# The rounded part and the rest of the softmax heads' norm factor, formed on GpSimd instead of VectorE

## The chip, the cores and the metric

The kernel runs on one core of one Trainium2 chip. The metric is device time of one execution in microseconds (us); lower is better. The engines are TensorE (PE in the profile; PEld is its weight load), VectorE (DVE), ScalarE (ACT), GpSimd (POOL) and SyncE (SP, which here only issues transfers). Each engine works through its own instructions in a fixed order.

## The reference, cut to what matters

Two layers over 512 tokens of width 1024. Each layer has eight stick-breaking heads and four heads of differential softmax attention side by side, then an output projection and an MLP with a squared ReLU. The part that matters here is the norm behind the four softmax heads:

```python
df_heads = differential_attention(dq, dk, dvv, lam)          # 4 heads of width 128
df_out = (rmsnorm(df_heads, subln_norm[l]) * (1.0 - lambda_init)).reshape(B, S, DF_WIDTH)
# rmsnorm: x * rsqrt(mean(x*x, axis=-1) + EPS) * g
```

and the rotation of the softmax heads' queries and keys, `rope`, which works in two halves of each head: one comes out as a difference of two products, the other as a sum.

## The kernel before, in words

**Layout and precision.** Activations stand transposed, channels on the 128 partitions and the 512 tokens along the row. Matmuls run in a rounded fp32 type (fp32r). To keep the precision, an operand is held as two tiles, a rounded part ("hi") and the rest ("lo"): ScalarE makes hi (`split`, L224; weights L116), VectorE subtracts it from the original to make lo (L225; weights L117). A dense product is then three matmuls (`three`, L281 to L283).

**Order of the work.** In each layer one stream of dense matmuls (the input projection, block after block, then the output projection of the softmax half) is interleaved on TensorE, in an order that is worked out when the program is built, with the attention pieces: the scores of one unit (L477, L478), the transposes of an older unit's weights (`s2`, L567) and the value products of a still older one (`s3`). TensorE takes them in exactly that order; a matmul whose operand is late holds up everything behind it. The framework's scheduler then places the instructions on the other engines by its own priorities, so that the order there is not always that of the source. The order on POOL is what matters below.

**The norm of a softmax head** (eight of them, heads 0 to 3 of two layers) has two halves. `start_norm` (L638) calls `rms_a` (L244) with GpSimd as `eng`: TensorE transposes the squares (L248); VectorE sums them (`ms`, L249) and adds the floor (L253); GpSimd raises the four columns to the power -1/2 (`rc`, L259, 128x4); VectorE rounds them (`chi`, L260) and subtracts (`clo`, L261); GpSimd spreads the columns onto two diagonals of 128x512 (`dghd`, L264, and `dgld`, L266). One stage later `finish` (L646) calls `rms_b`, where two matmuls broadcast the diagonals over the partitions (`rb_d`, L274 and L275), ScalarE copies the result (L276), and GpSimd multiplies the head's output by it (L650). `rms_a` is also called for the norm in front of the input projection, with VectorE as `eng`.

**The rotation of head 3** falls into the same stretch as the norm of an earlier head. VectorE multiplies the projection's result by cosines and sines (`u`, `v`, L445 and L446). GpSimd forms the sum (`v0d3q`, L454) and the difference (`u0d3q`, L453). Each is split (ScalarE L224 makes hi, VectorE L225 makes lo, both in tile `hl0d3k`), and SP moves the pieces by small transfers into the stacked operands of the scores (L420): hi into `st0d3k`, lo into `kl0d3k`, both into `st0d3q`. SP also issues the weight loads (L99) in its one order. In layer 1 the names have a 1 in place of the 0.

**Weights.** While TensorE works on a block, the next block's weights are split: ScalarE makes `whi` (L116), VectorE makes `wlo` (L117, 128x1024 from two tiles in SBUF).

Of the kernel before, what the change touches and what calls it, by code (L numbers as in the profile page):

```python
# [9 lines left out]
F32 = mybir.dt.float32  # L10
# [141 lines left out]
def trunk(ctx, tc, xT, w, w2, gains, gfin, lamv, cos, sin, out):  # L152
    nc = tc.nc
# [8 lines left out]
    def bank(tag, name):  # L162
        if tag == "any":
            tag = ("mm", "s", "s", "mm", "s")[turn[0] % 5]
            turn[0] += 1
        return ps.tile([P, 512], F32, tag=tag, name=name, bufs=banks[tag])
# [49 lines left out]
    chi = cp.tile([P, 4], F32R, tag="chi", name="chi")  # L216
    clo = cp.tile([P, 4], F32, tag="clo", name="clo")
# [26 lines left out]
    def rms_a(src, inv_n, col, name, eng, dgt, floor=None):  # L244
        pt = bank("t", "rs_" + name)
        if RST and eng is not nc.gpsimd or RST == 2:
            for j in range(4):
                nc.tensor.transpose(pt[:, j * P : (j + 1) * P], src[:, j * P : (j + 1) * P], ident)  # L248
            nc.vector.tensor_reduce(out=ms, in_=pt.rearrange("p (j f) -> p j f", j=4), axis=AX.X, op=ALU.add)  # L249
            if floor is None:  # L250
                nc.vector.tensor_scalar(out=ms, in0=ms, scalar1=inv_n, scalar2=EPS, op0=ALU.mult, op1=ALU.add)
            else:
                nc.vector.scalar_tensor_tensor(  # L253
                    out=ms, in0=ms, scalar=inv_n, in1=floor, op0=ALU.mult, op1=ALU.add)
        else:
            for j in range(4):
                nc.tensor.matmul(pt[:, j : j + 1], src[:, j * P : (j + 1) * P], ones, start=True, stop=True)
            nc.vector.tensor_scalar(out=ms, in0=pt[:, 0:4], scalar1=inv_n, scalar2=EPS, op0=ALU.mult, op1=ALU.add)
        nc.gpsimd.tensor_tensor(out=col, in0=ms, in1=mhalf, op=ALU.pow)  # L259
        nc.vector.tensor_copy(chi, col)  # L260
        nc.vector.tensor_sub(clo, col, chi.bitcast(F32))  # L261
        dg_hi, dg_lo = dgt("dgh" + name), dgt("dgl" + name)
        idb = ident.unsqueeze(1).to_broadcast([P, 4, P])
        eng.tensor_mul(  # L264
            dg_hi.rearrange("p (j t) -> p j t", j=4), idb, chi.bitcast(F32).unsqueeze(2).to_broadcast([P, 4, P]))
        eng.tensor_mul(  # L266
            dg_lo.rearrange("p (j t) -> p j t", j=4), idb, clo.unsqueeze(2).to_broadcast([P, 4, P]))

        return dg_hi, dg_lo
# [47 lines left out]
    for l in range(L):  # L317
        with ExitStack() as actx:
# [319 lines left out]
            def start_norm():  # L638
                b, os_, sqo, rc = late[0]
                floor = a3.tile([P, 4], F32, tag="floor", name=f"floor{l}{b}")  # L640
                nc.vector.scalar_tensor_tensor(
                    out=floor, in0=tops[b], scalar=EPS, in1=tops[b], op0=ALU.mult, op1=ALU.mult)
                dgs[b] = rms_a(sqo, 1.0 / P, rc, f"d{l}{b}", nc.gpsimd, tr, floor)
                return 0.43
# [65 lines left out]
            def dense(pts):  # L710
                if l == 0:
                    us = [W.next("x"), W.next("x")]
                    pts = [bank("mm", f"p{l}{i}") for i in range(2)]
                    turns = [(c, i) for c in range(5) for i in range(2)] + [(c, i) for i in range(2) for c in (5, 6, 7)]
                    for c, i in turns:
                        three(pts[i], wpair(us[i], c), hpair(c), c == 0, c == KC - 1)
                        yield 3 * 0.216
                step, b = 2 * KC, int(ORDER[0][1])
                held = [(pts[0], "d", b, "q"), (pts[1], "d", b, "k")]
                for item in ORDER[1:]:  # L720
                    kind, b = item[0], int(item[1])
                    for which in ("qk" if kind in "ds" else "v"):
                        name = f"p{l}{kind}{b}{which}"
                        for pt in block(name, "s" if step in (16, 24, 32) else "mm"):
                            step += 1
                            if step == RA[l]:
                                dgs["a"] = rms_a(ssq, 1.0 / D, rcol, f"a{l}", nc.vector, tr)
                            if step == RB[l]:
                                rms_b(rbc, f"a{l}", dgs["a"])
                                nc.vector.tensor_mul(cos_t, cos_t, rbc)  # L730
                                nc.vector.tensor_mul(sin_t, sin_t, rbc)
                            yield 3 * 0.216
                        held.append((pt, kind, b, which))
                        if step >= RB[l]:
                            for args in held:
                                {"w": evict_v, "u": evict_v, "s": evict_s, "d": evict_d}[args[1]](*args)
                            held = []
                yield from wo(1)
# [375 lines left out]
```

## Time and profile before

| what | us |
|---|---|
| median of 3 runs | 1173.97 |
| the 3 runs | 1173.69 to 1174.61 |
| the profiled execution, its own time | 1170.51 |
| its span, first to last instruction | 1168.7 |
| mean granted TensorE clock | 0.997 |

The span is what the views of the profile cover; 1.8 us of the profiled execution lie around it. A row of the timeline gives the start, the duration, engine, line, operation, what is written and what is read, shape and count, and, in brackets, how long the engine was idle just before and what ended that. An engine with a q behind its name (SPq) is the sequencer that issues a transfer. A row of the waits gives who waited for whom, the sum in us, the number of times and the longest.

### The profile page before, as it was taken

How to read it: one execution, taken by the hardware profiler on the slowest of the kernel's cores; microseconds unless marked ns; L12 is line 12 of the kernel's file. 1: busy time of each engine (PE TensorE's matmuls, PEld its weight loads, DVE VectorE, ACT ScalarE, POOL GpSimd, SP SyncE). 2: the span in 40 equal slices, each digit the busy share in tenths (PEclk: the TensorE clock that was granted, in tenths of full speed). 3: DMA queues.
4: the chain of work that ended last, by engine and by line, in shares of the span. 5: the costliest groups of instructions: out<-in, count | busy, mean ns of one | idle time of the engine just before them, and what ended most of it. 6: DMA issues, size and time to landing. Idle time of an engine off the chain costs nothing.

```text
span 1168.7 us, 15328 instructions
## 1 busy us (share of the span) xinstructions
PE 1147.7 (98%) x5454; PEld 952.0 (81%) x5454; DVE 813.0 (70%) x1302; ACT 652.4 (56%) x1153; POOL 213.7 (18%) x282
## 2 busy tenths in 40 slices
PE   9999999999999999999899999999999999999996
PEld 6887888888888888888688878888888888888884
DVE  7888788765545756647789877877655466476568
ACT  6455666556756446455445556655666563554554
POOL 1222443130100101002012215331201010010021
PEclk9999999999999999999999999999999999999999
DMA  7555433255844936837525553432658368276185
GB/s 246 163 151 171 123 113 109 72 190 152 212 136 105 224 128 126 224 95 157 110 72 166 168 153 109 140 96 73 225 122 229 120 124 226 93 168 192 36 173 132
DMA packets 56860, 170.11 MB, mean 146 GB/s; under 512 B 7120, under 2 KB 8144, under 8 KB 56784
## 3 DMA queue, kind: packets, MB, share of 16 engines
q1 hardware_dynamic: 46416, 131.88, 34.6%
q0 software_dynamic: 10224, 37.23, 18.5%
q8 instruction: 43, 0.70, 0.2%
q14 instruction: 33, 0.27, 0.1%
q10 hardware_dynamic: 144, 0.02, 0.0%
HBM read 138.17 MB, written 2.10 MB: 120 GB/s over the span
## 4 chain that ended last, share of the span: by engine, by line
PE 86%; DVE 5%; DMA 2%; issue 2%; ACT 1%; POOL 0%; SPq 0%; POOLq 0%; DVEq 0%; ACTq 0%
PE f L282 10%; PE f L283 10%; PE f L281 10%; PE x L282 4%; PE x L281 4%; PE x L283 4%; PE wo L281 3%; PE wo L282 3%; PE wo L283 3%; DMA q<-in_w 2%; DVE wlo L117 1%; PE T0s L567 1%; PE T1s L567 1%; PE O0s L596 0%; PE O1s L596 0%
## 5 line engine op out<-in xcount | busy, mean ns | idle before, releaser
L117 DVE TENSOR_TENSOR wlo<-raw,whi 128x1024 fp32r<-128x1024 f32 (+1 forms) x130 | 154.6, 1193 | 98.0 <-ACT whi L116 97.4
L117 DVE TENSOR_TENSOR wlo<-q,whi 128x512 fp32r<-128x512 f32 x224 | 146.0, 687 | 106.2 <-ACT whi L116 105.7
L281 PE MATMUL f<-h_hi,whi 128*128 128x512 f32 x512 | 199.6, 390 | 0.0
L283 PE MATMUL f<-h_hi,wlo 128*128 128x512 f32 x512 | 199.3, 389 | 0.0
L282 PE MATMUL f<-h_lo,whi 128*128 128x512 f32 x512 | 199.2, 389 | 0.0
L116 ACT ACTIVATE whi<-q 128x512 fp32r<-128x512 f32 x224 | 129.6, 624 | 120.3 <-PE f L282 38.1
L116 ACT ACTIVATE whi<-raw 128x1024 fp32r<-128x1024 f32 (+1 forms) x130 | 131.5, 1018 | 106.7 <-PE f L282 55.4
L794 POOL DMA_DIRECT2D q<-in_w x64 | 56.0, 878 | 558.1 <-DVE wlo L117 471.9
L281 PEld LDWEIGHTS f<-h_hi,whi 128*128 128x128 f32 x512 | 96.1, 188 | 19.9
L282 PEld LDWEIGHTS f<-h_lo,whi 128*128 128x128 f32 x512 | 96.1, 188 | 19.9
L283 PEld LDWEIGHTS f<-h_hi,wlo 128*128 128x128 f32 x512 | 96.1, 188 | 19.9
L225 DVE TENSOR_TENSOR Al<-F,Ah 128x256 fp32r<-128x256 f32 (+2 forms) x96 | 74.8, 779 | 44.1 <-ACT Ah L224 44.0
L281 PE MATMUL x<-whi,Ah 128*128 128x512 f32 x256 | 100.0, 391 | 0.0
L282 PE MATMUL x<-wlo,Ah 128*128 128x512 f32 x256 | 99.8, 390 | 0.1
L283 PE MATMUL x<-whi,Al 128*128 128x512 f32 x256 | 99.7, 389 | 0.0
L224 ACT ACTIVATE Ah<-F 128x256 fp32r<-128x256 f32 (+2 forms) x96 | 67.6, 704 | 45.7 <-DVE F L830 43.7
L282 PEld LDWEIGHTS x<-wlo,Ah 128*128 128x128 f32 x256 | 48.1, 188 | 10.4 <-DVE wlo L117 0.5
L281 PEld LDWEIGHTS x<-whi,Ah 128*128 128x128 f32 x256 | 48.1, 188 | 10.0
L283 PEld LDWEIGHTS x<-whi,Al 128*128 128x128 f32 x256 | 48.1, 188 | 9.9
L821 ACT ACTIVATE F<-f 128x512 f32<-128x512 f32 x64 | 37.6, 587 | 10.9 <-DVE Al L225 5.4
L822 ACT ACTIVATE F<-F 128x512 f32<-128x512 f32 x64 | 40.3, 630 | 1.5
L228 ACT ACTIVATE h_hi<-x,g_all 128x512 fp32r<-128x512 f32 x32 | 22.6, 718 | 26.1 <-DVE x L704 13.8
(1057 smaller groups left out, 2574.1 us busy)
## 6 DMA issues: line engine op xcount, KB each, us to landing
raw<-in_w SPq DMA_DIRECT2D x126, 512.0 KB, 3.5
q<-in_w SPq DMA_DIRECT2D x64, 512.0 KB, 5.5
q<-in_w POOLq DMA_DIRECT2D x64, 512.0 KB, 6.0
x<-in_xT SPq DMA_DIRECT2D x8, 256.0 KB, 4.3
raw<-in_w SPq DMA_DIRECT2D x8, 128.0 KB, 4.2
yx<-y POOLq DMA_DIRECT2D x2, 512.0 KB, 7.8
y<-y POOLq DMA_DIRECT2D x2, 512.0 KB, 7.7
y<-yx POOLq DMA_DIRECT2D x2, 512.0 KB, 6.0
```

The source lines that it names most:

```text
L116: h = nc.scalar.activation(hi[:, a:b], raw[:, a:b], AF.Copy)
L117: self.last = h, nc.vector.tensor_tensor(out=lo[:, a:b], in0=raw[:, a:b], in1=hi[:, a:b].bitcast(F32), op=ALU.subtract)
L224: nc.scalar.activation(hi, src, AF.Copy)
L225: nc.vector.tensor_tensor(out=lo, in0=src, in1=hi.bitcast(F32), op=ALU.subtract)
L228: a = nc.scalar.activation(h_hi[:, c, :], x[:, c, :], AF.Copy, scale=g)
L281: nc.tensor.matmul(pt, ah, bh, start=first, stop=False)
L282: nc.tensor.matmul(pt, ah, bl, start=False, stop=False)
L283: nc.tensor.matmul(pt, al, bh, start=False, stop=last)
L567: nc.tensor.transpose(pt[:, off : off + P], u["w"][qi][:, kb * P : (kb + 1) * P], ident)
L794: nc.gpsimd.dma_start(t, quad(g, q, c), accum_op=ALU.add)
L821: nc.scalar.activation(t, pt, AF.Relu)
L822: nc.scalar.activation(t, t, AF.Square)
```

## The change

In `rms_a` the two instructions that make the rounded part and the rest of the four columns go to the engine that was passed in, instead of always to VectorE. For the eight norms of the softmax heads that is GpSimd. For the two norms in front of the input projection it is VectorE, as before.

```diff
         nc.gpsimd.tensor_tensor(out=col, in0=ms, in1=mhalf, op=ALU.pow)
-        nc.vector.tensor_copy(chi, col)
-        nc.vector.tensor_sub(clo, col, chi.bitcast(F32))
+        eng.tensor_copy(chi, col)
+        eng.tensor_sub(clo, col, chi.bitcast(F32))
         dg_hi, dg_lo = dgt("dgh" + name), dgt("dgl" + name)
         idb = ident.unsqueeze(1).to_broadcast([P, 4, P])
         eng.tensor_mul(
```

## The prediction

> **What bounds the kernel now.** First the page: TensorE is busy for 98% of the span, and 86% of the chain that ended last is TensorE. The change touches no matmul, so it counts only where TensorE waits.
>
> ```profile
> span 1168.7 us, 15328 instructions
> PE 1147.7 (98%) x5454; PEld 952.0 (81%) x5454; DVE 813.0 (70%) x1302; ACT 652.4 (56%) x1153; POOL 213.7 (18%) x282
> PE 86%; DVE 5%; DMA 2%; issue 2%; ACT 1%; POOL 0%; SPq 0%; POOLq 0%; DVEq 0%; ACTq 0%
> ```
>
> Then the waits: two of TensorE's, and VectorE's for the power on GpSimd.
>
> ```profile
> PE S1d L477 <- DMA kl1d3k<-hl1d3k: 1.4, 1, 1.4
> ...
> PE S0d L477 <- issue: 1.4, 1, 1.4
> DVE chi L260 <- POOL rc L259: 9.2, 8, 1.7
> ```
>
> The eight waits of VectorE for GpSimd's power are what the change removes, 1.15 us each. Yet TensorE waits for none of these norms. Inside the attention it has two waits above 1 us, one a layer, both at the first scores of head 3 (L477). So I follow those two. In the timeline of TensorE:
>
> ```profile
> 96.63 0.36 PE L477 MATMUL S0d<-st0d3k,st0d3q 128*128 128x256 f32 x1 [1.35 <-issue]
> 674.76 0.36 PE L477 MATMUL S1d<-st1d3k,st1d3q 128*128 128x256 f32 x1 [1.37 <-DMA kl1d3k<-hl1d3k]
> ```
>
> In SP's timeline, and in the view of the tile `hl0d3k` for the landing time:
>
> ```profile
> 87.99 1.18 SPq L420 DMA_DIRECT2D st0d3k<-hl0d3k  x2
> 89.27 0.55 SPq L99 DMA_DIRECT2D raw<-in_w  x1
> 91.32 0.54 SPq L420 DMA_DIRECT2D st0d3q<-hl0d3k  x1
> ...
> 93.89 0.54 SPq L420 DMA_DIRECT2D st0d3q<-hl0d3k  x1
> ...
> DMA to landing us min/median/max: 2.6/2.7/2.8
> ```
>
> The scores need the fifth of the eight transfers that follow the weight load: 93.89 + 2.7 = 96.6, where TensorE starts. These eight go out back to back from 91.32, so their first sets the end of the wait. Layer 1 repeats it at 674.76, with a wait of 1.37 in place of 1.35. What sets 91.32? On VectorE and ScalarE:
>
> ```profile
> 82.58 0.67 DVE L446 TENSOR_TENSOR v0d3k<-p0d3k,sin_t 128x512 f32<-128x512 f32 x1
> 84.97 1.25 DVE L260 CAST chi<-rc 128x4 fp32r<-128x4 f32 x1 [1.72 <-POOL rc L259]
> 86.13 0.54 DVE L522 TENSOR_REDUCE sm0d<-S0d 128x1 f32<-128x384 f32 x1
> 86.60 0.75 DVE L261 TENSOR_TENSOR clo<-rc,chi 128x4 f32<-128x4 f32 x1
> 87.28 1.21 DVE L117 TENSOR_TENSOR wlo<-raw,whi 128x1024 fp32r<-128x1024 f32 x1
> ...
> 89.44 0.62 DVE L544 SCALAR_TENSOR_TENSOR p0d<-p0d,sm0d,p0d 128x384 f32<-128x384 f32 x1
> ...
> 90.58 0.68 DVE L225 TENSOR_TENSOR hl0d3k<-u0d3q,hl0d3k 128x512 fp32r<-128x512 f32 x1
> 81.56 1.06 ACT L116 ACTIVATE whi<-raw 128x1024 fp32r<-128x1024 f32 x1
> 87.34 0.62 ACT L224 ACTIVATE hl0d3k<-u0d3q 128x512 fp32r<-128x512 f32 x1
> ```
>
> The lo of the difference `u0d3q` ends at 90.58 + 0.68 = 91.26 and SP goes on at 91.32. It is late because VectorE stood at `chi` and `clo` and then had to catch up. SP itself was free at 89.82. So VectorE binds by 1.5 us, and the change would lift this, if nothing else moved.
>
> **The change part by part.** Something else moves: the order on GpSimd. With the four columns made there, the diagonals no longer wait for VectorE, and the scheduler puts them ahead of the difference of head 3. The order of the changed kernel on POOL, in both layers:
>
> ```
> before: L454 v, L259 rc, L453 u, L264 dghd, L266 dgld
> after:  L454 v, L259 rc, L260 chi, L261 clo, L264 dghd, L266 dgld, L453 u
> ```
>
> At the other six norms GpSimd's order stays but for the two new instructions; PE, ACT and SP issue theirs in the same order as before. GpSimd's rows in the profile of before:
>
> ```profile
> 82.65 1.30 POOL L454 TENSOR_TENSOR v0d3q<-v0d3q,u0d3k 128x512 f32<-128x512 f32 x1 [18.11 <-ACT whi L116]
> 83.90 1.03 POOL L259 TENSOR_TENSOR rc<-ms,mhalf 128x4 f32<-128x4 f32 x1
> 84.90 1.30 POOL L453 TENSOR_TENSOR u0d3q<-u0d3q,v0d3k 128x512 f32<-128x512 f32 x1
> 86.30 1.04 POOL L264 TENSOR_TENSOR dghd<-edge,chi 128x512 fp32r<-128x512 f32 x1
> 87.44 1.95 POOL L266 TENSOR_TENSOR dgld<-edge,clo 128x512 fp32r<-128x512 f32 x1
> ```
>
> *Removed.* On VectorE two small instructions and 1.15 us of idling at each of eight norms. At head 3 the stream behind `chi` can start near 83.25 (end of L446) in place of 86.13. Elsewhere TensorE has no wait to save, so this is worth nothing there. At head 3 it takes VectorE off the path, worth at most the two waits, 2 x 1.4 = 2.8 us.
>
> *Moved.* `u` now follows four instructions. Behind it stand ScalarE's hi, two transfers of it, the weight load, and then the eight. From the rows: hi 0.62, SP from 87.99 to 89.27 + 0.55 = 89.82, or 1.83, and some 0.12 for three hand-overs (87.34 + 0.62 = 87.96 to 87.99 is one). The first of the eight goes out 2.57 us after `u` ends. It equals 91.32 if `u` ends at 88.75. VectorE's lo (0.68, beside the 1.83) is hidden, since its stream has by then nothing else due. Every tenth by which `u` ends later adds a tenth to TensorE's wait, in each layer.
>
> *Added.* `chi` and `clo` on GpSimd, 128x4. No row shows them. Near rows, from the groups by line and form:
>
> ```profile
> L494 POOL MEMSET C0s<- 128x1 f32 x32 | 3.1, 98 | 1.7
> L498 POOL TENSOR_TENSOR sig0s<-sig0s,C0s 128x128 f32<-128x128 f32 x8 | 3.6, 445 | 11.8 <-DVE C0s L495 9.0 <-PE rb_d L275 1.4 <-PE T0s L567 0.8
> ```
>
> Bounds: 0.1 us each (a one-column fill) and 1.0 (the power on the same four columns). The subtraction's kind is the second row's, 0.45 at 128 columns against 1.04 at 512 (L264): 0.2 per 128, so about 0.25 at four. I take 0.25 each, hand-over included. [...]
>
> ```profile
> L260 DVE CAST chi<-rc x8: 169/170/1252, 85.0 to 724.9; 128x4 fp32r<-128x4 f32 x8
> ```
>
> Undisturbed, `u` ends at 83.90 + 1.00 (start to start) + 2 x 0.25 + 1.04 + 1.04 + 1.30 = 88.78: 0.03 late, no change.
>
> *Disturbed.* GpSimd and VectorE hold each other up where both work on tiles in SBUF. It is to be seen one head earlier, where L117 comes up during `v`, as it will here:
>
> ```profile
> 39.74 1.29 POOL L454 TENSOR_TENSOR v0d1q<-v0d1q,u0d1k 128x512 f32<-128x512 f32 x1 [3.56 <-issue]
> 40.12 1.99 DVE L117 TENSOR_TENSOR wlo<-raw,whi 128x1024 fp32r<-128x1024 f32 x1
> 40.99 2.27 POOL L453 TENSOR_TENSOR u0d1q<-u0d1q,v0d1k 128x512 f32<-128x512 f32 x1
> ```
>
> L117 waits until `v` ends at 41.03, then runs to 42.11, 1.08 us, and only then does GpSimd's next one get its 1.2 us: 2.27 in place of 1.30. In the same way `chi` (1.25, ending at 86.22 with `u`) and `dgld` (1.95, beside L117) were held in the rows above. Before, the stall at `chi` kept L117 back until the diagonals, which nothing waits for. Now L522 can run from 83.25 to 83.8 and L117 (its `whi` is done at 82.62) comes up about 83.7, while `v` runs to 83.95; it goes next, and the power, or `chi` behind it, stands back 1.08 us. Then L544, with two SBUF operands, falls due about 86.7, amid the diagonals. It takes 0.62, some 0.55 of it holding GpSimd. So `u` ends at 88.78 + 1.08 + 0.55 = 90.41, which is 1.66 after 88.75.
>
> *Sum.* 2 layers x 1.66 = 3.3 us: span 1168.7 to 1172.0, the profiled execution 1170.51 to 1173.8. The median of the runs lies 3.46 above that execution; as the wait is TensorE's own, I add the same to the median: 1173.97 + 3.3 = 1177.3.
>
> The other six norms stay covered. The tightest broadcast has this:
>
> ```profile
> 148.10 1.96 POOL L266 TENSOR_TENSOR dgld<-edge,clo 128x512 fp32r<-128x512 f32 x1
> 152.17 0.40 PE L275 MATMUL rb_d<-dgld,ones_r 128*128 128x512 f32 x1
> ```
>
> The diagonal is done at 150.06, 2.1 us ahead of its matmul. The two new instructions less VectorE's round trip (0.35 between power and diagonal at most norms) cost 0.15; one lock more costs 1.1.
>
> **The rivals.**
>
> *Undisturbed* (not slower): GpSimd's run of short instructions is let through, or is held once only. The place is `u` at head 3, the point of decision 88.75. With no lock the price is 0.03 a layer, 1174.0; with L117's alone 1.11, 1176.2. For it: the lock must meet instructions that before never stood side by side. Against it: 40.12, where the waiting L117 did go first.
>
> *Dear small instructions* (slower still): `chi` and `clo` cost more than 0.25 each, up to the power's 1.0, or another lock comes in. At 1.0, 2 x 0.75 a layer more, 3.0 us: 1180.3. For it: the power takes 1.0 for four columns. Against it: it is another operation, and L498's fit.
>
> *Freed VectorE* (faster): head 3's scores come without a wait, at 1173.97 - 2.8 = 1171.2. That needs `u` to end near 87.35, 1.4 before 88.75; the four instructions between the power and it would have to take 87.35 - 1.30 - 84.90 = 1.15 us together, and the two diagonals alone take 2.1. That the change doesn't free VectorE at all is not in question: the two instructions leave its list.
>
> **How the numbers follow.** About 0.2%, 2.3 us, is what a measurement here can tell from no change. Forecast, 1.2 to 2.2 us a layer (1176.4 to 1178.4): 0.50. Undisturbed, 1174.0 to 1176.3: 0.23. Dear, 1178.4 to 1180.3 and above: 0.24. Freed: 0.03. So faster 0.03, same 0.23, slower 0.74. The range leaves out the freed case, the lowest third of the undisturbed one (0.08) and a quarter of the dear one (0.06): 1174.6 to 1180.3.
>
> **What the profile after would show.** TensorE's wait at L477 of `S0d` and `S1d` near 3.0 us in place of 1.4; `u0d3q` (L453) behind `dgld`, ending near 90.4; VectorE's L117 close to 84 with the power or `chi` held beside it; `chi` and `clo` on GpSimd near 0.2 us; the first `st0d3q` issued near 93.0, set by SP's own row of issues and not by VectorE. It is wrong if L117 runs without holding GpSimd, if the small instructions cost 0.5 or more, or if TensorE has a new wait at `rb_d` or T0s.

## The result, and the profile after

| | before | after |
|---|---|---|
| median of 6 runs | 1173.83 (1170.33 to 1174.61) | 1181.53 (1179.28 to 1185.42) |
| the profiled execution, its own time | 1170.51 | 1182.46 |
| its span | 1168.7 | 1180.7 |
| mean granted TensorE clock | 0.997 | 0.990 |

The ratio is 1.0073 [1.0052, 1.0095]: slower by 7.7 us, where 3.3 were forecast, and beyond the range. The two profiled executions differ by more, 11.95 us, because the one of before lay 3.32 us under its median of six and the one of after lies 0.93 over its own: 11.95 - 3.32 - 0.93 = 7.70. Of all executions in this document one took 1383.99 us at a granted clock of 0.783 (in the run with 16 matmuls of zeros), and the figures of that run leave it out.

From the page of after, the lines that answer to those of before:

```profile
span 1180.7 us, 15326 instructions
...
PE   9998999999999999999899989999999999999996
...
PEclk9998999999999999999999989999999999999999
...
PE 82%; DVE 6%; DMA 3%; issue 2%; ACT 2%; POOL 2%; SPq 0%; POOLq 0%; DVEq 0%; ACTq 0%
```

The chain is less TensorE's own, 82% instead of 86%, with some 2% on GpSimd. A slice is 29.5 us long, so only a long stall dents one. Where TensorE waits is in the waits of after:

```profile
PE S1d L477 <- DMA kl1d3k<-hl1d3k: 5.3, 1, 5.3
PE S0d L477 <- DMA kl0d3k<-hl0d3k: 4.7, 1, 4.7
PE xT L863 <- DVE y L869: 2.0, 1, 2.0
...
PE rs_m L940 <- POOL ssq L238: 0.7, 1, 0.7
```

The first two are the same two places as before, head 3's first scores in each layer, with 5.3 and 4.7 us instead of 1.4 and 1.4. No new wait came up at `rb_d` or at T0s. The one at `rs_m`, a norm of another stage, is not among the waits of before; a second profile of the changed kernel (below) doesn't have it either. The third row is the longest wait of before, now shorter:

```profile
PE xT L863 <- DVE y L869: 3.2, 1, 3.2
```

The stretch ahead of head 3's scores in layer 0, in the timelines of after (POOL, DVE, ACT, SP's queue, PE):

```profile
82.90 1.30 POOL L454 TENSOR_TENSOR v0d3q<-v0d3q,u0d3k 128x512 f32<-128x512 f32 x1 [18.12 <-ACT whi L116]
84.16 2.01 POOL L259 TENSOR_TENSOR rc<-ms,mhalf 128x4 f32<-128x4 f32 x1
86.23 0.19 POOL L260 CAST chi<-rc 128x4 fp32r<-128x4 f32 x1
86.50 0.20 POOL L261 TENSOR_TENSOR clo<-rc,chi 128x4 f32<-128x4 f32 x1
86.65 1.07 POOL L264 TENSOR_TENSOR dghd<-edge,chi 128x512 fp32r<-128x512 f32 x1
87.69 1.35 POOL L266 TENSOR_TENSOR dgld<-edge,clo 128x512 fp32r<-128x512 f32 x1
89.01 1.29 POOL L453 TENSOR_TENSOR u0d3q<-u0d3q,v0d3k 128x512 f32<-128x512 f32 x1
...
83.88 1.40 DVE L117 TENSOR_TENSOR wlo<-raw,whi 128x1024 fp32r<-128x1024 f32 x1
...
86.86 1.29 DVE L544 SCALAR_TENSOR_TENSOR p0d<-p0d,sm0d,p0d 128x384 f32<-128x384 f32 x1
...
90.99 0.69 DVE L225 TENSOR_TENSOR hl0d3k<-u0d3q,hl0d3k 128x512 fp32r<-128x512 f32 x1 [2.25 <-ACT hl0d3k L224]
...
90.98 1.18 SPq L420 DMA_DIRECT2D st0d3k<-hl0d3k  x2
92.26 0.54 SPq L99 DMA_DIRECT2D raw<-in_w  x1
92.90 0.54 SPq L420 DMA_DIRECT2D st0d3q<-hl0d3k  x1
...
95.47 0.54 SPq L420 DMA_DIRECT2D st0d3q<-hl0d3k  x1
...
95.21 0.40 PE L283 MATMUL p0s0q<-h_hi,wlo 128*128 128x512 f32 x1
...
100.34 0.55 PE L477 MATMUL S0d<-st0d3k,st0d3q 128*128 128x256 f32 x1 [4.74 <-DMA kl0d3k<-hl0d3k]
```

Read it downwards. The difference `u0d3q` is last on GpSimd and ends at 90.30. VectorE is now idle ahead of its lo, which is done at 91.68; SP follows without a gap, from 90.98 to the first of the eight at 92.90. So far it is as forecast. The fifth of the eight goes out at 95.47, but it serves TensorE only at 100.34, 4.87 later. Before, that was 96.63 - 93.89 = 2.74. The scores start 3.71 us later: 1.58 from the later issue and 2.13 from the longer way. TensorE itself comes there 0.33 later (95.61 instead of 96.63 - 1.35 = 95.28), so its wait has grown by 3.38.

The view of the transfers has the reason for the longer way. Columns: issues in the stretch, size of each, median us from issue to landing. First before, from 89 to 99 us, then after, from 92 to 103:

```profile
raw<-in_w SPq DMA_DIRECT2D x2, 512.0 KB, 3.7
st0d3q<-hl0d3k SPq DMA_DIRECT2D x4, 128.0 KB, 2.7
kl0d3k<-hl0d3k SPq DMA_DIRECT2D x4, 128.0 KB, 2.8
```

```profile
raw<-in_w SPq DMA_DIRECT2D x2, 512.0 KB, 5.1
st0d3q<-hl0d3k SPq DMA_DIRECT2D x4, 128.0 KB, 5.0
kl0d3k<-hl0d3k SPq DMA_DIRECT2D x4, 128.0 KB, 4.9
```

The same eight transfers of the same size take 2.2 us more. What changed is the weight load of 512 KB ahead of them. Before, it went out at 89.27, 2.05 us ahead of the first of the eight, because these waited for VectorE's lo; after, it goes out at 92.26, 0.64 ahead. In layer 1 the eight take longer still, 5.8 us:

```profile
st1d3q<-hl1d3k SPq DMA_DIRECT2D x4, 128.0 KB, 5.8
```

Last the windows. Columns: stretch, its length, busy us and instructions of PE, PEld, DVE, ACT, POOL, the granted clock, the DMA engines' share, GB/s. First before, during the eight transfers and after the wait; then after, during the wait, behind it, and behind the wait of layer 1:

```profile
92.00:96.60 4.60, 3.28 (x17) 2.40 (x15) 4.52 (x10) 1.86 (x4) 0.00 (x0) 1.00 0.73 195
96.60:103.30 6.70, 6.67 (x37) 5.64 (x38) 4.36 (x10) 3.70 (x9) 1.29 (x1) 1.00 0.68 212
```

```profile
95.40:100.30 4.90, 0.21 (x1) 0.00 (x0) 1.57 (x3) 0.14 (x1) 0.00 (x0) 0.93 1.02 242
100.30:107.00 6.70, 6.66 (x22) 5.74 (x23) 3.93 (x8) 2.07 (x3) 0.00 (x0) 0.54 0.42 131
684.80:692.00 7.20, 7.20 (x26) 6.19 (x27) 4.22 (x8) 2.74 (x5) 0.01 (x1) 0.63 0.36 112
```

While TensorE waits, the DMA engines are full (1.02, against 0.73 before). Behind the wait TensorE is busy at about half its clock, 0.54 and 0.63, where before it had 1.00. If everything there ran slower in that proportion, it would cost (1 - 0.54) x 6.7 = 3.1 us and (1 - 0.63) x 7.2 = 2.7 us. What it did cost is read from the same matmuls in both profiles, from head 3's first scores to the third matmul of the value product behind them (L283). First before, then after:

```profile
102.26 0.28 PE L283 MATMUL O0d<-fh0d,vdl 128*128 128x256 f32 x1
```

```profile
108.65 0.28 PE L283 MATMUL O0d<-fh0d,vdl 128*128 128x256 f32 x1
```

That stretch took 102.26 - 96.63 = 5.63 us before and 108.65 - 100.34 = 8.31 after, 2.7 more. In layer 1 it took 680.44 - 674.76 = 5.68 and 692.73 - 684.78 = 7.95, 2.3 more.

So the 12.0 us between the profiled spans are made of: the wait in layer 0, 4.74 - 1.35 = 3.4; in layer 1, 5.34 - 1.37 = 4.0; the slower stretches behind the two, 2.7 and 2.3; the new wait at `rs_m`, 0.7; and L863, 3.17 to 2.04, -1.1. Together 12.0, to a tenth or two. (Why L863 came out shorter, and `rs_m` longer, was not followed up.)

### The profile page after: what moved, and what is told of

The parts are those of the page before. It is cut to its first block, busy times and chain, and to the rows that moved or that the text cites. A ratio compares the mean times of both kernels' runs of the same rounds, so it can differ in the third digit from the quotient of the medians.

```text
span 1180.7 us, 15326 instructions
## 1 busy us (share of the span) xinstructions
PE 1152.8 (98%) x5454; PEld 956.3 (81%) x5454; DVE 816.4 (69%) x1286; ACT 653.3 (55%) x1153; POOL 214.7 (18%) x298
## 4 chain that ended last, share of the span: by engine, by line
PE 82%; DVE 6%; DMA 3%; issue 2%; ACT 2%; POOL 2%; SPq 0%; POOLq 0%; DVEq 0%; ACTq 0%
PE f L281 10%; PE f L283 10%; PE f L282 10%; PE x L281 4%; PE x L282 4%; PE x L283 4%; PE wo L281 2%; PE wo L282 2%; PE wo L283 2%; DMA q<-in_w 2%; DVE wlo L117 1%; ACT whi L116 1%; PE T0s L567 1%; PE T1s L567 1%; PE O1s L596 0%
## 5 line engine op out<-in xcount | busy, mean ns | idle before, releaser
L117 DVE TENSOR_TENSOR wlo<-raw,whi 128x1024 fp32r<-128x1024 f32 (+1 forms) x130 | 157.3, 1214 | 93.4 <-ACT whi L116 92.7
L117 DVE TENSOR_TENSOR wlo<-q,whi 128x512 fp32r<-128x512 f32 x224 | 146.0, 687 | 107.9 <-ACT whi L116 107.5
L283 PE MATMUL f<-h_hi,wlo 128*128 128x512 f32 x512 | 199.3, 389 | 0.0
L283 PEld LDWEIGHTS f<-h_hi,wlo 128*128 128x128 f32 x512 | 96.1, 188 | 20.0
L283 PE MATMUL x<-whi,Al 128*128 128x512 f32 x256 | 99.7, 389 | 0.0
L283 PEld LDWEIGHTS x<-whi,Al 128*128 128x128 f32 x256 | 48.1, 188 | 10.0
```

What stands on the lines that cost most here:

```text
L117: self.last = h, nc.vector.tensor_tensor(out=lo[:, a:b], in0=raw[:, a:b], in1=hi[:, a:b].bitcast(F32), op=ALU.subtract)
L283: nc.tensor.matmul(pt, al, bh, start=False, stop=last)
```

## The experiments

The theory after this result: GpSimd's order makes `u` late; then SP issues the load and the eight back to back, and the eight land 2 us later for it; the long wait costs clock besides. The rivals: the instructions on GpSimd cost by themselves, at any norm; or the longer landing comes from `u` being late at all, and not from the load just ahead. Times below are medians, with the lowest and the highest run in brackets; the ratio is to the kernel before on the same chip. The edits shift line numbers by a few lines.

### `u` put ahead of the two instructions

Against after; head 3's difference keeps the place on GpSimd that it had before, ahead of the diagonals. Nothing else changes.

```diff
-        eng.tensor_copy(chi, col)
+        small[:] = [eng.tensor_copy(chi, col)]
...
-                    nc.gpsimd.tensor_sub(u1, u1, v)
+                    diff = nc.gpsimd.tensor_sub(u1, u1, v)
+                    if b == 3:
+                        behind(small[0], diff)
```

> The changed kernel with one thing put back: on GpSimd the difference of head 3 (u, L453 of before) stands ahead of chi, clo and the diagonals again, as it did before the change; chi and clo stay on GpSimd at all eight norms. Theory (the place of u does it: head 3's transfers go out late, just behind a weight load, land late, and TensorE waits 4.7 and 5.3 us at L477 and then runs at a low clock): u ends near 87.3 instead of 90.3, the wait at head 3's scores is 1 to 2 us a layer, no low clock behind it, 1172 to 1176 us. Rival (the two small instructions cost by being on GpSimd, at all eight norms): the time stays within 2 us of the changed kernel, 1179 to 1183.

Measured: 1175.28 (1171.3 to 1179.22, 12 runs), ratio 1.0014 [1.0000, 1.0027]. The order on GpSimd is worth most of the loss: 1.0073 falls to 1.0014. But not all goes, and the landing stays long: the waits are 2.2 and 2.3 us, where 1 to 2 were expected. From this kernel's timeline and its transfers from 90 to 100 us:

```profile
90.10 0.54 SPq L99 DMA_DIRECT2D raw<-in_w  x1
90.74 0.54 SPq L422 DMA_DIRECT2D st0d3q<-hl0d3k  x1
...
98.46 0.55 PE L481 MATMUL S0d<-st0d3k,st0d3q 128*128 128x256 f32 x1 [2.22 <-DMA st0d3q<-hl0d3k]
```

```profile
st0d3q<-hl0d3k SPq DMA_DIRECT2D x4, 128.0 KB, 5.1
```

The first of the eight leaves at 90.74, ahead of the 91.32 of before, and still the scores start later (98.46 against 96.63): with the load 0.64 us ahead, the eight take 5.1. So the long landing doesn't need a late `u`. Layer 1 has a like wait, 2.3. In the windows behind the two waits the clock fell in layer 0 only, to 0.76, where no fall was looked for:

```profile
98.00:105.00 7.00, 6.54 (x27) 5.63 (x28) 4.22 (x8) 2.95 (x7) 0.22 (x1) 0.76 0.49 131
679.70:686.70 7.00, 6.54 (x37) 5.67 (x38) 4.39 (x9) 3.64 (x9) 1.30 (x1) 1.00 0.51 155
```

The stretch from the scores to that matmul of the value product took 105.53 - 98.46 = 7.07 us in layer 0 and 685.74 - 680.16 = 5.58 in layer 1, so this one fall cost 1.5 us. The profile also has a wait of 2.0 us for `whi` at an `x` (L283), which neither before nor after has; it was not followed up, and may account for a part of the loss that is left.

### The weight load earlier on SP

Against after; the one load L99 that stands ahead of the eight goes ahead of head 3's second hi transfer. `u` stays late.

```diff
-            self.nc.sync.dma_start(t, self.dram[self.loaded])
+            got = self.nc.sync.dma_start(t, self.dram[self.loaded])
+            while self.hold:
+                self.hold.pop()(got)
...
-                                move(k[half][to, m, :], ...)
+                                moved = move(k[half][to, m, :], ...)
+                                if b == 3 and j == 0 and half == 0:
+                                    W.hold.append(lambda got, moved=moved: behind(moved, got))
```

> The changed kernel with one thing moved on SP: the weight load that goes out just ahead of head 3's eight transfers goes out ahead of the two transfers of u's hi, so some 5 us earlier (one of these two then goes out between the eight); the order on all other engines is the changed kernel's. Theory (the eight land after 5 us instead of 2.7 because they share the DMA engines with that load): landing falls back to 2.6 to 3.0 us, the wait at L477 to 2.0 to 2.8 us a layer, no low clock, 1175 to 1177 us. Rival (the long landing has another cause, and the wait comes from u alone): landing stays near 5, and the time near 1181.

Measured: 1175.51 (1172.94 to 1178.61, 12 runs), ratio 1.0017 [1.0006, 1.0028]. In the timeline the load is 5.58 us ahead of the first of the eight; in the view of the transfers these land in 2.6 again:

```profile
86.59 0.54 SPq L99 DMA_DIRECT2D raw<-in_w  x1
...
92.17 0.54 SPq L422 DMA_DIRECT2D st0d3q<-hl0d3k  x1
```

```profile
st0d3q<-hl0d3k SPq DMA_DIRECT2D x4, 128.0 KB, 2.6
```

The waits are 2.1 and 1.9 us, with `u` ending at 90.72, as late as in after. The load no longer stands between the hi transfers and the eight, so these also leave 1.45 us after `u` instead of 2.60, with one hi transfer now among them. Behind the wait of layer 0 the clock fell here too, where none was expected; behind that of layer 1 it stayed at 1.00:

```profile
98.00:105.00 7.00, 6.91 (x29) 5.81 (x30) 4.22 (x8) 3.31 (x8) 0.58 (x1) 0.76 0.62 191
```

The rival that a late `u` makes the landing long falls from both sides: in the first experiment it is early and the landing long, here it is late and the landing short. And each half of the theory is worth most of the loss by itself: the late `u` and the load just ahead are bad together, and the clock can fall behind what either makes (0.76 behind the wait of layer 0 in both runs).

### Head 0's norm left on VectorE

Against after; only the norm beside head 3's rotation, one of four in each layer, has `chi` and `clo` on VectorE as before. The other six keep them on GpSimd.

```diff
-        eng.tensor_copy(chi, col)
-        eng.tensor_sub(clo, col, chi.bitcast(F32))
+        fine = nc.vector if name[-1] == "0" else eng
+        fine.tensor_copy(chi, col)
+        fine.tensor_sub(clo, col, chi.bitcast(F32))
```

> The change at six of the eight norms: only the norm of head 0, whose instructions meet the rotation of head 3, makes chi and clo on VectorE as before, in both layers. Theory (only the meeting with u matters): 1173 to 1175 us, as before, waits of 1.4 us at L477. Rival (each norm's share is the same): six eighths of 7.7 us stay, 1179 to 1180.

Measured: 1172.69 (1168.84 to 1175.13, 12 runs), ratio 0.9992 [0.9978, 1.0005], a little under the 1173 to 1175 expected; head 3's waits are 1.5 and 1.6. The rival that the instructions cost by themselves falls: at six of the eight norms they cost nothing that can be measured.

### The order alone, with the two instructions on VectorE

Against before; nothing is moved to GpSimd, only `u` is put behind the low diagonal.

```diff
-        eng.tensor_mul(
-            dg_lo..., idb, clo...)
+        small[:] = [eng.tensor_mul(
+            dg_lo..., idb, clo...)]
...
+                    diff = nc.gpsimd.tensor_sub(u1, u1, v)
+                    if b == 3:
+                        behind(diff, small[0])
```

> The kernel before, with the order alone: chi and clo stay on VectorE, but on GpSimd u stands behind both diagonals, as in the changed kernel. Theory (the place of u does it): u ends 2.5 us or more later than before, the wait at L477 is 3 to 6 us a layer with a low clock behind it, 1178 to 1184 us. Rival (the engine of the two instructions does it): no more than 2 us over the kernel before, 1174 to 1176.

Measured: 1178.81 (1176.72 to 1183.35, 6 runs), ratio 1.0052 [1.0035, 1.0070]. The order alone makes most of the loss. The two layers differ, and that is a control that came by chance: in layer 1 the scheduler itself put the load ahead of the hi transfers. The waits and the transfers, layer 0 (from 91 to 101 us) and layer 1:

```profile
PE S0d L481 <- DMA st0d3q<-hl0d3k: 4.6, 1, 4.6
...
PE S1d L481 <- DMA kl1d3k<-hl1d3k: 1.9, 1, 1.9
```

```profile
st0d3q<-hl0d3k SPq DMA_DIRECT2D x4, 128.0 KB, 5.1
...
st1d3q<-hl1d3k SPq DMA_DIRECT2D x4, 128.0 KB, 2.8
```

One kernel, the same late `u` in both layers: with the load 0.65 us ahead (91.75, then 92.40) it lands in 5.1 and the wait is 4.6; with the load earlier 2.8 and 1.9. (With the load out of the row the first of the eight also leaves earlier after `u`, so the landing, and not the wait alone, is what to compare.)

### Both edits together, on the change

Against after; the first edit and the second at once, in short:

```diff
+                    if b == 3:
+                        behind(small[0], diff)
...
+                                if b == 3 and j == 0 and half == 0:
+                                    W.hold.append(lambda got, moved=moved: behind(moved, got))
```

> The changed kernel with both edits: u of head 3 ahead of chi, clo and the diagonals on GpSimd, and the weight load ahead of u's two transfers on SP. Theory (u's place makes the transfers late by 1.3 us, sharing with the load by another 2.3): u ends near 88, the decisive transfer lands 7.4 us later as in the run with the load alone moved, near 95.4, which is ahead of TensorE's need; the wait at head 3's scores is under 0.6 us a layer, and the time falls below the kernel before, 1170 to 1172 us. Rival (something else then binds those scores, VectorE's lo above all): the wait stays at 1 us or more, and the time at the kernel before's, 1173 to 1174.

Measured: 1169.47 (1167.74 to 1170.67, 6 runs), ratio 0.9959 [0.9946, 0.9972]. It beats both kernels; against the one before on its chip it is 0.41% faster, 4.5 us between the medians (1174.0), and so a little faster than expected. Head 3's wait is gone in both layers; from the timeline:

```profile
86.58 0.55 SPq L99 DMA_DIRECT2D raw<-in_w  x1
...
90.18 0.54 SPq L424 DMA_DIRECT2D st0d3q<-hl0d3k  x1
...
96.17 0.35 PE L485 MATMUL S0d<-st0d3k,st0d3q 128*128 128x256 f32 x1 [0.22 <-ACT vdh L397]
```

### The load earlier, on the kernel before

Against before; the second edit alone:

```diff
+                                if b == 3 and j == 0 and half == 0:
+                                    W.hold.append(lambda got, moved=moved: behind(moved, got))
```

> The kernel before with the weight load alone moved ahead of u's two transfers on SP. Theory (before, the eight transfers wait for VectorE's lo, held at chi and clo, and land without the load in their way): no change, the wait stays 1.3 to 2.0 us a layer, 1172.5 to 1174.5 us, so that the gain of the run with both edits needs the two instructions off VectorE. Rival (the load's place alone gives the gain): 1170 to 1172 us.

Measured: 1176.03 (1172.99 to 1182.1, 12 runs), ratio 1.0023 [1.0006, 1.0040]; waits 1.9 and 2.1. The time is above the 1172.5 to 1174.5 expected. Behind the wait of layer 1 the clock was lower: 0.79 from 676 to 684 us. Without the change the early load helps nothing and costs a little: VectorE's lo still sets the first of the eight (91.15), behind this stall in the timeline, and one hi transfer now stands among the eight.

```profile
84.80 1.25 DVE L262 CAST chi<-rc 128x4 fp32r<-128x4 f32 x1 [1.72 <-POOL rc L261]
```

So the gain of both edits needs the two instructions off VectorE.

### TensorE kept busy in the wait

Against after; 16 matmuls on zeros, whose result is overwritten, stand ahead of head 3's first scores, so that TensorE isn't idle there. Their place in the order is pinned.

```diff
+                        if b == 3 and i == 0 and m == 0:
+                            for _ in range(16):
+                                nc.tensor.matmul(both, zeros[:, 0:128], zeros[:, 128:640], start=True, stop=True)
```

> The changed kernel with 16 matmuls of zeros in front of head 3's first scores in both layers, into the bank that the scores then overwrite: TensorE works some 3.5 us of its wait; the order on the other engines is the changed kernel's, on TensorE one pair of scores stands ahead of three transposes instead of behind. Theory (some 3 us a layer are lost behind the wait, since the granted clock falls to 0.5 to 0.6 for 7 us after it): with a wait of 1 to 2 us left, the clock stays near 1.0 in one or both layers, and the time falls by 2 to 6 us to 1175 to 1179. Rival (the low clock does not come from TensorE's idling, or costs nothing on the path): the time stays within 1.5 us of the changed kernel's, 1180 to 1183.

Measured: a median of 1181.87 (1176.96 to 1183.33, 5 runs), ratio 1.0056 [1.0036, 1.0077], where 1175 to 1179 was expected. The clock behind the wait did stay at 1.00 in both layers, with 1.1 and 1.0 us of the wait left:

```profile
96.00:103.00 7.00, 5.87 (x30) 3.59 (x29) 2.55 (x5) 2.07 (x3) 0.00 (x0) 1.00 0.76 181
684.00:692.00 8.00, 8.00 (x45) 6.87 (x44) 5.71 (x16) 5.50 (x14) 1.29 (x1) 1.00 0.47 133
```

So in this profile the low clock goes when TensorE isn't idle there. But the time came out where the rival put it, as if the clock cost nothing in the median. The next two runs, on one chip, are the change with 22 such matmuls and the change unedited.

```diff
-                            for _ in range(16):
+                            for _ in range(22):
```

> The changed kernel once more, unedited, on the chip of the next run, to have its waits, its clock and its time beside that one. 1179 to 1184 us, waits of 4 to 5.5 us at head 3's scores in both layers, mean granted clock 0.990 to 0.993.

> The changed kernel with 22 matmuls of zeros in front of head 3's first scores, some 4.7 us, in place of 16: the whole wait is covered in most executions. Theory (the fall of the clock behind the wait costs some 4 us over both layers, by the mean granted clock of 0.9925 against 0.996): the clock is back at 0.995 or more, and the time 2 to 5 us below the changed kernel's of the same call. Rival (what the clock shows costs nothing, since TensorE's order is held up by other engines in that stretch anyway): clock back, but the time within 1.5 us of the changed kernel's.

Measured: the change 1181.8 (1180.71 to 1185.63, 6 runs), ratio 1.0071 [1.0055, 1.0087], waits 4.7 and 4.5; with 22 fillers 1180.4 (1178.38 to 1183.16), ratio 1.0050 [1.0035, 1.0064]. The clock is at 1.00 behind the place in both layers again. The scores came as late as without fillers (100.15 in layer 0, against 100.42), so that the clock alone differs there. No wait is left at head 3, but another has grown, from 2.2 in the run beside it, and `rs_m` has two of 0.7 that the run beside it doesn't have:

```profile
PE xT L877 <- DVE y L883: 4.5, 1, 4.5
```

The 1.4 us between them are less than the 2 to 5 expected, and the two intervals overlap: the rival's side once more. What the low clock costs in the median stays open between nothing and some 4 us, the second worked out from the mean granted clocks of the runs, 0.9925 for after and 0.996 with the fillers: 0.0035 x 1175.

## Why the prediction was wrong in size

**Right.** The place: beside the two waits at head 3's scores no wait of TensorE grew by more than 0.7 us (`rs_m`), and the other six norms cost nothing that can be measured (head 0 left on VectorE: 0.9992). The order: `u` is last on GpSimd, and the order alone makes 1.0052 of the 1.0073. The small instructions: 86.17 to 86.65 for both, 0.48, where 0.5 was taken; so *Dear small instructions* falls. The cast took 0.19 here and the subtraction 0.20 (medians of eight); on VectorE in before the cast took 0.17 in the median, and the subtraction 0.16 at its shortest. The first of the eight: 2.60 us after `u` ends (90.30 to 92.90; 2.57 was worked out), set by SP's own row.

**The locks**, nearly. (The word stands for what the rows show: an instruction of one engine takes longer beside one of the other.) The power took 2.01 instead of 1.03 beside L117, and the low diagonal 1.35 instead of 1.04 beside L544: 0.98 + 0.31 = 1.29, where 1.08 + 0.55 was forecast. (In layer 1 it was `u` itself that stood beside L544, 1.61 instead of 1.28.) In before the same is seen of L117, 1.99 beside `v` of head 1 and 1.21 alone (at 93.69), and not of L446, which reads the matmuls' result: 0.68 beside that `v`, 0.67 beside head 3's and 0.68 alone (at 74.6). Against *Undisturbed*, the two rows of after show that both locks came; what it is that holds GpSimd in them was not shown. In all, from the start of `v` to the first of the eight 8.67 us became 10.00: 1.33 late, where 1.66 was forecast.

**The step that failed** is "Every tenth by which `u` ends later adds a tenth to TensorE's wait", with the fifth transfer's "93.89 + 2.7 = 96.6" behind it: the landing was taken as a constant. It was 2.7 with the eight standing back behind VectorE's lo, the first of them 2.05 us behind the load, and 5.0 with 0.64 us between them. The forecast itself said that SP would now set the first of the eight, which is to say that load and eight go out back to back; I read that only as a time of issue. It cost 2.13 us in layer 0, more than the 1.58 that the issue came later. The load early (2.6), the two layers of the order alone (5.1 and 2.8) and both edits together show that the load just ahead does it.

An estimate from these rows says why all eight are late alike. They are issued one every 0.64 us, 128 KB / 0.64 us = 205 GB/s, about what the DMA engines moved in these stretches (195 to 242). A load of 512 KB ahead takes 512 KB / 242 GB/s = 2.2 us, and such a backlog isn't made up while the eight follow at the same rate. That the longer way is the queue of just these bytes is argued, not shown; that it goes with the load's lead is shown.

**The term that was missing** is the clock, which the sum put at nothing. It let TensorE go on at full speed behind a longer wait. In after, waits of 4.7 and 5.3 us were followed by 0.54 and 0.63. A shorter wait can do it and need not: in the first experiment one of 2.22 us in layer 0 was followed by 0.76, and one of 2.31 in layer 1 by 1.00. With the landing in the sum, the forecast would have had 3.4 + 4.0 = 7.4 us of waits, and so 1181.4 without the clock. The median came out there, at 1181.53; but the profiled execution has the clock's 2.7 + 2.3 = 5.0 us on top, and how the median's 7.7 divides between waits, clock and the rest stays open, as the fillers left it.

**Freed VectorE** was held for nearly excluded, since GpSimd's order forbade it. With that order and SP's undone it is what happens: 4.5 us under before, where 2.8 was worked out for it. The profiles show the waits go (0.2 us is left at head 3's scores in each layer, and those of layer 0 start at 96.17 instead of 96.63), but not where the rest of the 4.5 comes from: the mean granted clock of that execution is 0.995, where before has 0.997, and its span, 1168.9, ends level with before's 1168.7.

## What to carry to other kernels

Where a transfer stands behind a wait, ask what else is on its queue: here the stall that kept the eight back also put 2.05 us between them and a load of 512 KB, and with the stall gone, 0.64 us behind that load, they took 5.0 us to land instead of 2.7. The freed engine was worth 4.5 us with the orders on GpSimd and SP set by hand (1169.47 against 1174.0) and nothing without them (1181.53 against 1173.83), so look at the changed order first, and put the late instruction ahead by hand. A wait on TensorE may cost clock behind it as well: here the clock was 0.76 to 0.79 behind waits of 1.9 to 2.2 us in some places and stayed at 1.00 behind 1.9 to 3.2 in others, so a small delay isn't linear in the time.

## What the runs showed of the hardware

- The eight 128 KB moves between tiles took 2.6 to 2.8 us (medians) when the 512 KB load on the same queue went out 2 us or more ahead, and 4.9 to 5.1 (5.6 and 5.8 in layer 1 of after) when it went out 0.64 or 0.65 ahead; the load itself 5.1 instead of 3.7.
- GpSimd's cast and subtraction of 128x4 took 0.19 and 0.20 us (medians of eight; single ones up to 0.99, and in the first experiment 0.52); a power of the same shape took 1.03, and 2.01 beside VectorE's L117.
- In the first experiment the clock fell behind one wait of 2.2 us (0.76 in the 7 us that followed) and stayed at 1.00 behind one of 2.3, in one and the same execution. It fell likewise behind 1.9 us (the order alone, layer 1: 0.76) and 2.1 (the early load, on after in layer 0, 0.76, and on before in layer 1, 0.79 from 676 to 684), and stayed behind 1.9 in the other layer of each of these last two, and behind the 3.2 of L863 in before (1.00 from 1143 to 1150 us).
